# A two-block transformer kernel with 32 experts: a branch that falls through, one more early fetch of rows, four slot tables for sixteen

## The chip, the cores and the metric

The kernel runs on one core of a Trainium2 chip. A core has five engines, each with its own instruction stream: TensorE (PE) for matrix products, VectorE (DVE), ScalarE (ACT), GpSimd (POOL) and SyncE (SP), which here only starts transfers. Sixteen DMA engines carry the transfers of all queues. A transfer can be put on a hardware queue (by SP or ACT) or on the software queue (by POOL). The metric is device time in microseconds (us), the median of several runs; less is better.

## The reference

Two blocks follow each other on 512 tokens of width 1024. The first is a mixer (sparse attention and a gated MLP) with a feed-forward layer; the second has a differential attention, a mixture of experts and a gated embedding. The change touches the mixture of experts and what follows it:

```python
def moe(xn, w_router, b_router, w_gate, b_gate, w_up, b_up, w_down, b_down):
    logits = (xt @ w_router).astype(jnp.float32) + b_router.astype(jnp.float32)
    top_vals, top_idx = lax.top_k(logits, TOP_K)
    gates = jax.nn.softmax(top_vals, axis=-1).astype(xn.dtype)
    ...
    def expert_block(args):
        xb, e = args
        gt = xb @ w_gate[e] + b_gate[e]
        up = xb @ w_up[e] + b_up[e]
        gt = jnp.minimum(gt, SWIGLU_LIMIT)
        up = jnp.clip(up, -SWIGLU_LIMIT, SWIGLU_LIMIT)
        hdn = (up + 1.0) * (gt * jax.nn.sigmoid(SWIGLU_ALPHA * gt))
        return hdn @ w_down[e] + b_down[e]
    ...
h = h + moe(rms_norm_2(h, ffn_norm[i]), ...)
gate = jax.nn.sigmoid(rms_norm_2(h, ple_gate_norm[i]) @ w_ple_gate[i])
e = rms_norm_2(p[i] @ w_ple_proj[i], ple_post_norm[i])
h = h + gate * e
```

Every expert has three 1024x1024 float32 matrices, 12 MB in all, so the experts' weights are 384 MB.

## The kernel before

**The routing.** From about 900 us the kernel chooses the experts. The experts are worked through as 32 places; places 0 to 2 are experts 0 to 2, the later ones are ordered by how many tokens they have. Each place takes the rows of its tokens into a tile `xg` by an indirect DMA of POOL (`gather`, L1499). For the first three places the token numbers are found by a product with a one-hot matrix (`one_hot`, `slot_products`, `tokens_of`). Place 0 reads its rows from `base`, the rows before the norm, and DVE scales them afterwards (`scale_rows`); place 1 reads from `normed`, which holds the scaled rows and whose last quarter is written late (`store_normed(0)`). For the other 29 places POOL scatters one entry for each token and each of its four choices into tables in memory (`scatter_entries`, L1578): 16 indirect DMAs of 128 entries, each into a table of its own. Later ACT loads the 16 tables back (`table_slots`, L1768, 64 KB each), and DVE adds them (`sum_tables`, L1774).

**The stream of weights.** `seq` lists 768 steps (matrix, place, k) of 512 KB of weights. SP loads two steps at a time (1 MB, L1545) into one of ten raw buffers; for each step ACT rounds the weights to a high part `whi` and DVE computes the rest `wlo` (both L297), each into a slot of a ring. PE then makes three products a step (L326 to L328, two matmuls of 512 columns each), or two where the place has at most 64 tokens (L1733, L1734). `fetch(i + 6)` stands ahead of step i, so the splits run about five steps ahead. A raw buffer is loaded again when its second `wlo` is done. The order of PE, DVE, ACT and POOL is the order of the program; `put(i, f)` hangs a piece of other work `f` on step i. SP's loads go in order too, and each load also waits until the hardware semaphore that it will signal is free again. There are eight of these (DMAHW0 to 7 in the lists below), taken in turn by all hardware transfers, SP's and ACT's.

```python
for i, (n, p, k) in enumerate(seq):
    fetch(i + 1 + SPLIT_AHEAD)
    for f in beside[i]:
        f()
    ...
```

`begin[1]` is 16, so before the change the table loads hang on steps 24 to 27, the sums on 32, 33 and 34; `turn_rows(1)`, which turns the rows of place 1 on PE (L1703), hangs on step 10.

**Behind the experts.** A place takes at most 112 rows. Where an expert has more, a general path (a loop with branches over all experts, `tc.If(any_over > 0)`, L2111) computes the rest; with these inputs it is never taken. Behind it stands the last stage: SP loads the experts' results (`yb`, L2128), POOL and DVE add them to the rows (`first_sums`, `pair_up`, `add_rows`), PE multiplies by the gate's weights `w_pg`, which SP loaded before the branch (L2023, 512 KB each, eight of them).

Of the kernel before, what the change touches and what calls it, by code (L numbers as in the profile page):

```python
# [21 lines left out]
P = 128  # L22
S = 512
D = 1024
NT = 4
# [214 lines left out]
def build(tc, I, out, dbg=None, stop=None):  # L240
# [3 lines left out]
    with es:  # L244
# [558 lines left out]
        def attention(g, fill):  # L803
# [7 lines left out]
            for i in range(len(units) + AHEAD):  # L811
# [4 lines left out]
                if i in fill:  # L816
# [20 lines left out]
                  {forward - 1: [f"g{i}" for i in range(3)], mixer - 1: [f"p{i}" for i in range(5)], experts - 1: ['x0', 'x1', 'e0']}, {"g": mixer - 1, "p": mixer + 3}, mixer)  # L837
# [434 lines left out]
        tables = [dram.tile([P * NE, 4], F32, name=f"table{j}") for j in range(4 * NT)]  # L1272
# [201 lines left out]
        nc.gpsimd.memset(lower[0:P - SMALL].bitcast(F32), 0.0)  # L1474
# [8 lines left out]
        slots = {}  # L1483

# [13 lines left out]
        def gather(p, src, m, ap):  # L1498
            nc.gpsimd.indirect_dma_start(out=xg[:m], out_offset=None, in_=src, in_offset=bass.IndirectOffsetOnAxis(ap=ap, axis=0),  # L1499
                                         bounds_check=S - 1, oob_is_err=False)  # L1500
# [75 lines left out]
        def scatter_entries(js):  # L1576
            for j in js:
                nc.gpsimd.indirect_dma_start(out=tables[j], out_offset=bass.IndirectOffsetOnAxis(ap=place[:, j // 4, j % 4:j % 4 + 1], axis=0), in_=entry[:, j // 4, j % 4], in_offset=None,  # L1578
                                             bounds_check=P * NE - 1, oob_is_err=False)
# [45 lines left out]
        slot_products(ptok, oh0, (1, 2, 3), 4, told)  # L1625
        weigh(2)
# [11 lines left out]
        gi0 = tokens_of(ptok, 0)  # L1638

        gather(0, base, CAP, gi0)  # L1640
        norm0 = early.tile([P, 4], F32, name="norm0")[:CAP]
        nc.vector.tensor_copy(norm0, ptok[:CAP, 0:4])
        nc.vector.tensor_tensor(out=norm0[:, 3:4], in0=norm0[:, 1:2], in1=norm0[:, 2:3], op=ALU.add)
# [119 lines left out]
        def table_slots(q):  # L1763

            if q == 0:
                sums.extend(row_tile("tabs").rearrange("p (j f) -> p j f", j=8) for _ in range(2))
            for j in range(4 * q, 4 * q + 4):
                nc.scalar.dma_start(sums[j // 8][:, j % 8], tables[j].rearrange("(s e) c -> s (e c)", e=NE))  # L1768

        sums = []  # L1770

        def sum_tables(h):
            tab = tabs[h] = row_tile("tab")[:, :4 * NE].rearrange("p (e c) -> p e c", c=4) if h else early.tile([P, NE, 4], F32, name="tab")
            nc.vector.reduce_sum(tab.rearrange("p e c -> p (e c)"), sums[h].rearrange("p j f -> p f j"), axis=AX)  # L1774
# [3 lines left out]
        def all_slots():  # L1778
            tab = tabs[0]
            nc.vector.tensor_tensor(out=tab, in0=tab, in1=tabs[1], op=ALU.add)  # L1780
# [12 lines left out]
        def turn_rows(p):  # L1793
            pts["x", p] = turned(xg, cap[p])
# [124 lines left out]
        put(11, split_rows, 1)  # L1919
        put(14, gates_by_expert)  # L1920
# [45 lines left out]
        scatter_entries(range(15, 10, -1))  # L1966
# [3 lines left out]
        gather(1, normed, CAP, gi1)  # L1970
        scatter_entries(range(10, -1, -1))
# [139 lines left out]
        with tc.If(any_over > 0):  # L2111
            with tc.tile_pool(name="op", bufs=1, side="right") as op:
                with tc.For_i(0, NE) as e:
                    n_e = nc.values_load(count[0:1, bass.ds(e, 1)], min_val=0, max_val=S, skip_runtime_bounds_check_because="a count of 512 tokens at most")
                    for r in range(-(-(S - SMALL) // P)):
                        with tc.If(n_e > P * r):
                            overflow_rows(op, e, r)


        with pool("fin", 2, side="right") as wp:  # L2120
# [30 lines left out]

            def add_rows(tt):
                h, yb = hs[tt], ybs[tt]
                for cs in pieces(tt):
                    pair_up(tt, cs)
# [56 lines left out]
            for tt in range(NT):  # L2212
                ps = ps_pair()
                if tt == 0:
# [3 lines left out]
                    for c in range(4):  # L2218
# [10 lines left out]
                    turn_rows_of(1)  # L2229
# [48 lines left out]
```

## Time and profile before

| | us |
|---|---|
| median of 3 runs | 2075.75 (2075.34 to 2076.8) |
| profiled execution, whole | 2073.2 |
| profiled execution, span from first to last instruction | 2071.5 |
| PE busy | 1968.3 (95%) |
| DVE busy | 1640.3 (79%) |
| ACT busy | 1370.9 (66%) |
| mean granted clock of PE | 0.985 of full speed |

The span is one execution under the profiler; 1.7 us of that execution lie around it. Busy shares are means over stages with different limits: the expert stage, from about 930 to 1990 us, is half of the time, and most of the change lies at its two ends.

### The profile page before, as it was taken

How to read it: one execution, taken by the hardware profiler on the slowest of the kernel's cores; microseconds unless marked ns; L12 is line 12 of the kernel's file. 1: busy time of each engine (PE TensorE's matmuls, PEld its weight loads, DVE VectorE, ACT ScalarE, POOL GpSimd, SP SyncE). 2: the span in 40 equal slices, each digit the busy share in tenths (PEclk: the TensorE clock that was granted, in tenths of full speed). 3: DMA queues.
4: the chain of work that ended last, by engine and by line, in shares of the span. 5: the costliest groups of instructions: out<-in, count | busy, mean ns of one | idle time of the engine just before them, and what ended most of it. 6: DMA issues, size and time to landing. Idle time of an engine off the chain costs nothing. (4 is left out here: it accounts for less than half of the span.)

```text
span 2071.5 us, 28687 instructions
## 1 busy us (share of the span) xinstructions
PE 1968.3 (95%) x9675; PEld 1507.0 (73%) x9676; DVE 1640.3 (79%) x2290; ACT 1370.9 (66%) x1889; POOL 414.6 (20%) x363
## 2 busy tenths in 40 slices
PE   8999999999999888878999999999999999999968
PEld 6777779888878887666777777777667766767546
DVE  6688874223466666678999999999999999999965
ACT  5656753222355364537799988888888888888942
POOL 0100120000010334124223444322211003201122
PEclk9999999999999998989999999999999999999989
DMA  5510464233555402248999999999999999999973
GB/s 215 173 31 22 176 230 154 91 102 102 182 202 191 129 11 72 107 173 338 403 410 406 412 406 407 402 404 402 405 396 403 399 398 402 398 407 398 365 270 106
DMA packets 113158, 554.16 MB, mean 268 GB/s; under 512 B 16739, under 2 KB 25955, under 8 KB 63852
## 3 DMA queue, kind: packets, MB, share of 16 engines
q1 hardware_dynamic: 90528, 510.04, 63.6%
q10 hardware_dynamic: 15116, 25.40, 3.6%
q0 software_dynamic: 7360, 16.82, 2.4%
q8 instruction: 78, 1.28, 0.2%
q14 instruction: 76, 0.62, 0.1%
HBM read 532.62 MB, written 26.66 MB: 270 GB/s over the span
## 5 line engine op out<-in xcount | busy, mean ns | idle before, releaser
L297 DVE TENSOR_TENSOR wlo<-wraw,whi 128x1024 fp32r<-128x1024 f32 x923 | 1076.1, 1215 | 209.4 <-ACT whi L297 203.8
L297 ACT CAST whi<-wraw 128x1024 fp32r<-128x1024 f32 x923 | 923.1, 1049 | 217.2 <-PE po L327 28.0
L1715 POOL DMA_INDIRECT ybuf<-yt,si x31 | 190.6, 6150 | 453.4 <-ACT yt L1820 453.4
L326 PE MATMUL pw<-whi,xe 128*112 128x512 f32 x544 | 215.9, 397 | 0.0
L327 PE MATMUL pw<-wlo,xe 128*112 128x512 f32 x544 | 214.4, 394 | 0.1
L328 PE MATMUL pw<-whi,xe 128*112 128x512 f32 x544 | 214.0, 393 | 0.0
L1734 PE MATMUL pw<-wlo,xe 128*64 128x512 f32 x406 | 162.9, 401 | 8.6 <-DVE wlo L297 8.0
L1733 PE MATMUL pw<-whi,xe 128*128 128x512 f32 x406 | 161.3, 397 | 3.2 <-DVE xe L297 3.2
L332 POOL TENSOR_SCALAR rstd<-ss 128x1 f32<-128x1 f32 (+1 forms) x68 | 24.8, 364 | 626.9 <-DVE ss L877 387.5
L326 PE MATMUL pw<-whi,he 128*112 128x512 f32 x320 | 128.1, 400 | 0.0
L1499 POOL DMA_INDIRECT xg<-normed,gi x31 | 62.5, 2017 | 327.2 <-PE tr L1703 284.8
L327 PE MATMUL pw<-wlo,he 128*112 128x512 f32 x320 | 126.4, 395 | 0.2
L328 PE MATMUL pw<-whi,he 128*112 128x512 f32 x320 | 126.2, 394 | 0.0
L328 PEld LDWEIGHTS pw<-whi,xe 128*112 128x112 f32 x544 | 94.7, 174 | 31.6
L326 PEld LDWEIGHTS pw<-whi,xe 128*112 128x112 f32 x544 | 94.7, 174 | 31.2
L327 PEld LDWEIGHTS pw<-wlo,xe 128*112 128x112 f32 x544 | 94.8, 174 | 30.9 <-DVE wlo L297 0.7
L1733 PEld LDWEIGHTS pw<-whi,xe 128*128 128x128 f32 x406 | 76.4, 188 | 34.2 <-DVE xe L297 3.6
L1734 PEld LDWEIGHTS pw<-wlo,xe 128*64 128x64 f32 x406 | 54.5, 134 | 46.4 <-DVE wlo L297 31.1
L1733 PE MATMUL pw<-whi,he 128*128 128x512 f32 x182 | 74.1, 407 | 0.0
L1734 PE MATMUL pw<-wlo,he 128*64 128x512 f32 x182 | 72.9, 401 | 0.0
L326 PE MATMUL pa<-x2T,whi 128*128 128x512 f32 (+1 forms) x200 | 72.6, 364 | 0.1
L327 PE MATMUL pa<-x2T,whi 128*128 128x512 f32 (+1 forms) x200 | 72.6, 363 | 0.0
(617 smaller groups left out, 4212.7 us busy)
## 6 DMA issues: line engine op xcount, KB each, us to landing
wraw<-in_we_gate_dram SPq DMA_DIRECT2D x128, 1024.0 KB, 20.4
wraw<-in_we_up_dram SPq DMA_DIRECT2D x128, 1024.0 KB, 21.5
wraw<-in_we_down_dram SPq DMA_DIRECT2D x128, 1024.0 KB, 20.4
wraw<-in_w_gu_dram SPq DMA_DIRECT2D x44, 512.0 KB, 3.8
wraw<-in_w_down_dram SPq DMA_DIRECT2D x44, 512.0 KB, 4.5
wraw<-in_w_out_dram SPq DMA_DIRECT2D x24, 512.0 KB, 5.6
yb<-ybuf SPq DMA_DIRECT2D x6, 1024.0 KB, 8.7
wraw<-in_w_v_dram SPq DMA_DIRECT2D x10, 512.0 KB, 3.9
```

Source lines behind the costliest of these rows:

```text
L297: return nc.scalar.copy(hi, src), nc.vector.tensor_tensor(out=lo, in0=src, in1=hi.bitcast(F32), op=ALU.subtract)
L326: nc.tensor.matmul(o, a[0], b[0], start=start, stop=False)
L327: nc.tensor.matmul(o, a[0], b[1], start=False, stop=False)
L328: W["mm"] = nc.tensor.matmul(o, a[1], b[0], start=False, stop=stop)
L332: ins = nc.gpsimd.tensor_scalar(out=r[:, :w], in0=ss, scalar1=1.0 / n, scalar2=eps, op0=ALU.mult, op1=ALU.add)
L1499: nc.gpsimd.indirect_dma_start(out=xg[:m], out_offset=None, in_=src, in_offset=bass.IndirectOffsetOnAxis(ap=ap, axis=0), bounds_check=S - ...
L1715: nc.gpsimd.indirect_dma_start(out=ybuf, out_offset=bass.IndirectOffsetOnAxis(ap=ap, axis=0), in_=y_, in_offset=None, bounds_check=4 * S - ...
L1733: nc.tensor.matmul(ps[:, cs], a[:, k, 0:P], hi, start=first, stop=False)
L1734: nc.tensor.matmul(ps[:m, cs], a[:, k, 0:m], lo, start=False, stop=False)
```

## The change

Five edits come together.

1. The two tables of the scatters: 16 tables become 4, scatter j writes into table j % 4 (each token has a place of its own in each, so nothing is overwritten but zeros). All 16 scatters stand in one row, ahead of place 0's products. The four tables are loaded by POOL, hung on step 20, and summed by one reduction at step 26.
2. The rows of place 1 are gathered right behind those of place 0, from `base`, into a tile `x1` of their own, and scaled on DVE. Their one-hot matrix lies in the tile `lower`, whose clearing moves to step 12.
3. The room for `x1` is a slot of the ring of split weights (`e0`), which then has one slot less.
4. `tc.If` is told not to prefer its body as the block that follows directly.
5. In the last stage POOL's first additions of a tile (`pair_rows`) stand a tile ahead, and the turning of tile 1's rows stands behind the loads.

```diff
-                  {forward - 1: ..., experts - 1: ['x0', 'x1', 'e0']}, ...
+                  {forward - 1: ..., experts - 1: ['x0', 'x1']}, ...
...
-        tables = [dram.tile([P * NE, 4], F32, name=f"table{j}") for j in range(4 * NT)]
+        tables = [dram.tile([P * NE, 4], F32, name=f"table{j}") for j in range(4)]
...
-        nc.gpsimd.memset(lower[0:P - SMALL].bitcast(F32), 0.0)
+        x1 = W["e0"].tile([P, D], F32, name="x1")
+        nc.gpsimd.memset(x1, 0.0)
...
+        def fetched(p):
+            return x1 if p == 1 else xg
...
+        oh1, ptok1, told1 = lower[:, :NT * CAP].rearrange("p (t c) -> p t c", c=CAP), ps_tr(1), []
+        one_hot(slot_of[:, :, 1:2], (1, 2, 3), oh1)
+        slot_products(ptok1, oh1, (1, 2, 3), 4, told1)
...
         one_hot(slot_of[:, :, 0:1], (0,), oh0)
+        one_hot(slot_of[:, :, 1:2], (0,), oh1)
         slot_products(ptok, oh0, (0,), 4, told)
+        slot_products(ptok1, oh1, (0,), 4, told1)
...
-        gather(0, base, CAP, gi0)
...
+        gis = [tokens_of(ptok, 0), tokens_of(ptok1, 1)]
+        norms_of = []
+        for p, pt in enumerate((ptok, ptok1)):
+            gather(p, base, CAP, gis[p])
...
         places()
-        oh1, ptok1 = new_one_hot(), ps_tr(1)
-        one_hot(slot_of[:, :, 1:2], range(NT), oh1)
-        slot_products(ptok1, oh1, range(NT), 2, [])
-        gi1 = tokens_of(ptok1, 1)
         fetch(2)
-        for cs in (slice(0, 512), slice(512, D)):
-            scale_rows(xg[:CAP, cs], xg[:CAP, cs], norm0[:, 3:4], gpre[:CAP, cs])
+        for p in range(2):
+            x = fetched(p)[:CAP]
+            for cs in (slice(0, 512), slice(512, D)):
+                scale_rows(x[:, cs], x[:, cs], norms_of[p][:, 3:4], gpre[:CAP, cs])
...
+        def load_tables():
+            rows["tabs"] = row_tile("tabs")[:, :16 * NE].rearrange("p (j f) -> p j f", j=4)
+            for j in range(4):
+                nc.gpsimd.dma_start(rows["tabs"][:, j], tables[j].rearrange("(s e) c -> s (e c)", e=NE))
...
+        put(12, lambda: nc.gpsimd.memset(lower[0:P - SMALL].bitcast(F32), 0.0))
...
-        for q in range(4):
-            put(begin[1] + 8 + q, table_slots, q)
-        for h in range(2):
-            put(begin[1] + 16 + h, sum_tables, h)
+        put(20, load_tables)
+        put(begin[1] + 10, sum_tables)
         put(begin[1] + 18, all_slots)
...
-        scatter_entries(range(15, 10, -1))
+        scatter_entries(range(15, -1, -1))
         keep_warm(10, bias[:, 0:P], bias[:, 0:512])
         turn_rows(0)
         split_rows(0)
-        gather(1, normed, CAP, gi1)
-        scatter_entries(range(10, -1, -1))
...
-        with tc.If(any_over > 0):
+        with tc.If(any_over > 0, preferred_fallthrough_block=False):
...
+                            pair_rows(1)
                             sums[1] = on_chip_rows(1)
                             add_rows(1)
...
+                if tt + 2 < NT:
+                    pair_rows(tt + 2)
+                if tt == 0:
+                    turn_rows_of(1)
```

**POOL around the first gathers.** In the lists below each row is a line of the program, an operation, what it writes and reads, and the semaphores that it waits for (DMASW0 to 7 are those of POOL's own transfers, DMAHW0 to 7 those of SP's and ACT's). Before, from the gather of place 0 on:

```order
L1499 DMA xg<-base,gi_9002 112x1024 [waits DMAHW5_49,DMAHW7_49,DMAHW2_49,DVE_49]
L1578 DMA table_8109<-entry,place 4096x4 [waits DVE_49]
L1578 DMA table_8108<-entry,place 4096x4 [waits DMAHW4_49]
L1578 DMA table_8107<-entry,place 4096x4 [waits DMAHW3_49]
L1578 DMA table_8106<-entry,place 4096x4
L1578 DMA table_8105<-entry,place 4096x4 [waits DMAHW1_49]
L1499 DMA xg<-normed,gi_9035 112x1024 [waits DMAHW1_49,DMAHW0_49,DMAHW3_49,DMASW0_49,DMAHW5_49,DVE_49,PE_49]
L1578 DMA table_8104<-entry,place 4096x4
L1578 DMA table_8103<-entry,place 4096x4
L1578 DMA table_8102<-entry,place 4096x4 [waits DMASW1_49]
L1578 DMA table_8101<-entry,place 4096x4 [waits DMASW2_49]
```

After, from the same gather on (`x_8621` is `x1`):

```order
L1503 DMA xg<-base,gi_8986 112x1024 [waits DMAHW3_49,DMAHW6_49,DMAHW1_49,DVE_49]
L1503 DMA x_8621<-base,gi_8990 112x1024 [waits DVE_49]
L1582 DMA table_8097<-entry,place 4096x4 [waits DVE_49]
L1582 DMA table_8096<-entry,place 4096x4 [waits DMAHW0_49]
L1582 DMA table_8095<-entry,place 4096x4
L1582 DMA table_8094<-entry,place 4096x4
L1582 DMA table_8097<-entry,place 4096x4 [waits DMASW2_49]
L1582 DMA table_8096<-entry,place 4096x4 [waits DMASW3_49]
L1582 DMA table_8095<-entry,place 4096x4 [waits DMASW4_49,DMASW0_49]
L1582 DMA table_8094<-entry,place 4096x4 [waits DMASW5_49,DMASW1_49]
L1582 DMA table_8097<-entry,place 4096x4 [waits DMASW6_49]
L1582 DMA table_8096<-entry,place 4096x4 [waits DMASW7_49]
```

The gather of place 1 moved up from behind five scatters to directly behind the first, and reads `base`. Each scatter from the fifth on now waits for the landing of the scatter four ahead of it, which wrote the same table. The row goes on after the change to the gather of place 2 and the table loads:

```order
L1582 DMA table_8095<-entry,place 4096x4 [waits DMASW4_49]
L1582 DMA table_8094<-entry,place 4096x4 [waits DMASW5_49]
L1925 MEMSET lower 64x1024 [waits PE_49]
L1503 DMA xg<-normed,gi_9221 112x1024 [waits DMAHW4_49,DMAHW5_49,DMAHW1_49,DMAHW7_49,DVE_49,PE_49]
L1776 DMA tabs<-table_8094 128x128 [waits DMASW1_49]
L1776 DMA tabs<-table_8095 128x128 [waits DMASW0_49]
L1776 DMA tabs<-table_8096 128x128 [waits DMASW7_49]
L1776 DMA tabs<-table_8097 128x128 [waits DMASW6_49]
```

The four table loads stand between the gathers of places 2 and 3, each behind the last scatter into its table.

**SP around the branch.** L2111 is `tc.If` before, L2113 after; `most` is the count on which it branches. Before:

```order
L2023 DMA wraw<-in_w_pg_dram 128x1024 [waits DMAHW5_49,PE_49]
L2023 DMA wraw<-in_w_pg_dram 128x1024 [waits DMAHW6_49,DVE_49,PE_49]
L2110 TENSOR_LOAD most [waits DVE_49]
L2111 COMPARE_AND_BRANCH
...
L2111 UNCONDITIONAL_BRANCH [waits SP_sequencer_49,DMAHW0_49,DMAHW1_49,DMAHW2_49,DMAHW3_49,DMAHW4_49,DMAHW5_49,DMAHW6_49,DMAHW7_49]
L2128 DMA yb<-ybuf 128x4x256 [waits DMASW3_49,DMASW4_49,DMASW2_49,DMASW5_49,DMASW1_49,DMASW6_49,DMASW0_49,DMASW7_49,DVE_49,DMAHW7_49,PE_49,Activation_49]
```

The branch jumps over the general path, some 220 rows left out at the dots, to a block that waits for all eight hardware semaphores. After:

```order
L2025 DMA wraw<-in_w_pg_dram 128x1024 [waits DMAHW0_49,PE_49]
L2025 DMA wraw<-in_w_pg_dram 128x1024 [waits DMAHW1_49,DVE_49,PE_49]
L2112 TENSOR_LOAD most [waits DVE_49]
L2113 COMPARE_AND_BRANCH
L2113 UNCONDITIONAL_BRANCH [waits SP_sequencer_49,DMAHW0_49,DMAHW1_49,DMAHW2_49,DMAHW3_49,DMAHW4_49,DMAHW5_49,DMAHW6_49,DMAHW7_49]
...
L2025 DMA wraw<-in_w_pg_dram 128x1024 [waits DMAHW2_49,PE_49]
L2130 DMA yb<-ybuf 128x4x256 [waits DMASW3_49,DMASW4_49,DMASW2_49,DMASW5_49,DMASW1_49,DMASW6_49,DMASW0_49,DMASW7_49,DVE_49,DMAHW3_49,PE_49,Activation_49]
```

The waiting block now follows the branch directly, and ends in an unconditional branch over the general path, the same rows left out at the dots. One load of `w_pg` that stood ahead of the branch now stands behind it, ahead of the first `yb`. PE, DVE, ACT and POOL have the same two branches in the same order, with their own part of the general path between.

## Rows read from the trace of the kernel before

**Rows 1.** page, part 1, of TensorE
```profile
PE 1968.3 (95%) x9675; PEld 1507.0 (73%) x9676; DVE 1640.3 (79%) x2290; ACT 1370.9 (66%) x1889; POOL 414.6 (20%) x363
```

**Rows 2.** windows of the expert stage: engines' busy time, granted clock, DMA share, GB/s
```profile
1000.00:1200.00 200.00, 200.00 (x925) 145.91 (x924) 199.19 (x191) 178.75 (x200) 75.00 (x13) 1.00 1.01 406
...
1400.00:1600.00 200.00, 196.30 (x886) 139.57 (x885) 191.67 (x183) 172.54 (x191) 36.56 (x12) 1.00 1.01 401
```

**Rows 3.** timeline of PE: start, us, what, idle before and its releaser
```profile
927.57 0.99 PE L1703 MATMUL tr<-ident,xg 112*128 112x112 f32 x8
...
938.87 0.52 PE L1495 MATMUL tr<-info,oh 128*112 128x2 f32 x4 [2.69 <-DVE oh L1488]
...
951.35 1.73 PE L1703 MATMUL tr<-ident,xg 112*128 112x112 f32 x8 [4.46 <-DMA xg<-normed,gi]
...
955.04 0.40 PE L326 MATMUL pw<-whi,he 128*112 128x512 f32 x1
955.28 0.40 PE L327 MATMUL pw<-wlo,he 128*112 128x512 f32 x1
```

**Rows 4.** timeline of DVE, same stretch and columns
```profile
925.17 1.40 DVE L352 SCALAR_TENSOR_TENSOR xg<-xg,norm,g_ffn_norm 112x512 f32<-112x512 f32 x2
...
952.94 1.37 DVE L297 TENSOR_TENSOR xe<-tr,xe 128x448 fp32r<-128x448 f32 x2 [3.71 <-ACT xe L297]
```

**Rows 5.** timeline of POOL, same columns
```profile
921.28 1.12 POOL L1578 DMA_INDIRECT table<-entry,place  x1 [4.03 <-DVE place L1574]
...
937.10 5.93 POOL L1499 DMA_INDIRECT xg<-normed,gi  x1 [8.48 <-DVE wlo L297]
943.33 1.09 POOL L1578 DMA_INDIRECT table<-entry,place  x1 [0.30 <-issue]
...
959.27 1.44 POOL L1578 DMA_INDIRECT table<-entry,place  x1 [0.30 <-issue]
```

**Rows 6.** line L1578, the scatters: time from issue to landing
```profile
DMA to landing us min/median/max: 2.1/6.1/8.3
```

**Rows 7.** windows of the dip and of the stretch behind it
```profile
960.00:990.00 30.00, 30.00 (x140) 22.86 (x139) 28.11 (x36) 21.02 (x24) 1.73 (x2) 1.00 0.80 286
1000.00:1050.00 50.00, 50.00 (x233) 36.76 (x232) 49.94 (x49) 41.68 (x47) 12.61 (x3) 1.00 1.01 404
```

**Rows 8.** waits of SP, 955 to 985: us, times, longest
```profile
SPq L1545 <- DMA tabs<-table: 17.2, 3, 10.7
```

**Rows 9.** timeline of DVE, the table sums
```profile
987.15 1.98 DVE L1774 TENSOR_REDUCE tab<-tabs 128x128 f32<-128x1024 f32 x1
```

**Rows 10.** page, part 6: DMA issues, KB each, median us to landing
```profile
wraw<-in_we_gate_dram SPq DMA_DIRECT2D x128, 1024.0 KB, 20.4
...
wraw<-in_w_gu_dram SPq DMA_DIRECT2D x44, 512.0 KB, 3.8
```

**Rows 11.** DMA issues from 1004 to 1046, same columns
```profile
wraw<-in_we_gate_dram SPq DMA_DIRECT2D x8, 1024.0 KB, 9.0
```

**Rows 12.** line L2111, the branch: ns min/median/max, first and last start
```profile
L2111 SPq EVENT_SEMAPHORE  x9: 17/17/17, 1988.7 to 1993.7; - x9
...
L2111 ACTq EVENT_SEMAPHORE  x2: 17/17/17, 1990.3 to 1990.4; - x2
...
L2111 SPq COMPARE_BRANCH  x1: 50/50/50, 1982.3 to 1982.3; - x1
L2111 PEldq COMPARE_BRANCH  x1: 7026/7026/7026, 1987.0 to 1987.0; - x1
...
L2111 ACTq COMPARE_BRANCH  x1: 45/45/45, 1988.8 to 1988.8; - x1
```

**Rows 13.** timeline of SP behind the branch
```profile
1994.60 2.96 SPq L2128 DMA_DIRECT2D yb<-ybuf  x4
```

**Rows 14.** windows around the branch
```profile
1990.00:1995.00 5.00, 0.53 (x1) 0.50 (x2) 1.64 (x2) 2.47 (x3) 0.00 (x0) 0.50 0.27 98
```

**Rows 15.** timeline of POOL in the last stage
```profile
2025.20 6.65 POOL L2150 TENSOR_TENSOR yb<-yb 128x512 f32<-128x512 f32 x4
```

More of the change, by code (lines that the diff above doesn't have):

```diff
@@ L836, in build @@
         open_ring("ring2", stages + ["h"] * (NE * 24), lambda u: 2 if u < experts - 1 else SPLIT_AHEAD if u >= experts else 0,
-                  {forward - 1: [f"g{i}" for i in range(3)], mixer - 1: [f"p{i}" for i in range(5)], experts - 1: ['x0', 'x1', 'e0']}, {"g": mixer - 1, "p": mixer + 3}, mixer)
+                  {forward - 1: [f"g{i}" for i in range(3)], mixer - 1: [f"p{i}" for i in range(5)], experts - 1: ['x0', 'x1']}, {"g": mixer - 1, "p": mixer + 3}, mixer)
         if stop == "mix":
@@ L1498, in gather @@
         def gather(p, src, m, ap):
-            nc.gpsimd.indirect_dma_start(out=xg[:m], out_offset=None, in_=src, in_offset=bass.IndirectOffsetOnAxis(ap=ap, axis=0),
+            nc.gpsimd.indirect_dma_start(out=fetched(p)[:m], out_offset=None, in_=src, in_offset=bass.IndirectOffsetOnAxis(ap=ap, axis=0),
                                          bounds_check=S - 1, oob_is_err=False)
@@ L1577, in scatter_entries @@
             for j in js:
-                nc.gpsimd.indirect_dma_start(out=tables[j], out_offset=bass.IndirectOffsetOnAxis(ap=place[:, j // 4, j % 4:j % 4 + 1], axis=0), in_=entry[:, j // 4, j % 4], in_offset=None,
+                nc.gpsimd.indirect_dma_start(out=tables[j % 4], out_offset=bass.IndirectOffsetOnAxis(ap=place[:, j // 4, j % 4:j % 4 + 1], axis=0), in_=entry[:, j // 4, j % 4], in_offset=None,
                                              bounds_check=P * NE - 1, oob_is_err=False)
@@ L1637, in build @@
             nc.tensor.matmul(pn, ones, chosen[:, t2], start=t2 == 0, stop=t2 == NT - 1)
-        gi0 = tokens_of(ptok, 0)
-        gather(0, base, CAP, gi0)
-        norm0 = early.tile([P, 4], F32, name="norm0")[:CAP]
-        nc.vector.tensor_copy(norm0, ptok[:CAP, 0:4])
-        nc.vector.tensor_tensor(out=norm0[:, 3:4], in0=norm0[:, 1:2], in1=norm0[:, 2:3], op=ALU.add)
+        gis = [tokens_of(ptok, 0), tokens_of(ptok1, 1)]
+        norms_of = []
+        for p, pt in enumerate((ptok, ptok1)):
+            gather(p, base, CAP, gis[p])
+            t = early.tile([P, 4], F32, name=f"norm{p}")[:CAP]
+            nc.vector.tensor_copy(t, pt[:CAP, 0:4])
+            nc.vector.tensor_tensor(out=t[:, 3:4], in0=t[:, 1:2], in1=t[:, 2:3], op=ALU.add)
+            norms_of.append(t)
         weigh(0)
@@ L1761, in fold_lower, with sum_tables @@
                 W["mm"] = nc.tensor.matmul(ps[:SMALL, cs], fold, lower[:, cs], start=False, stop=True, skip_group_check=True)
[L1763 to L1774, printed above, removed]
+        def load_tables():
+            rows["tabs"] = row_tile("tabs")[:, :16 * NE].rearrange("p (j f) -> p j f", j=4)
+            for j in range(4):
+                nc.gpsimd.dma_start(rows["tabs"][:, j], tables[j].rearrange("(s e) c -> s (e c)", e=NE))
+        def sum_tables():
+            tab = tabs[0] = early.tile([P, NE, 4], F32, name="tab")
+            nc.vector.reduce_sum(tab.rearrange("p e c -> p (e c)"), rows.pop("tabs").rearrange("p j f -> p f j"), axis=AX)
         tabs = {}
@@ L1779, in all_slots @@
             tab = tabs[0]
-            nc.vector.tensor_tensor(out=tab, in0=tab, in1=tabs[1], op=ALU.add)
             gi, si = rows_of(early, tab[:, :, 1], tab[:, :, 2], NE)
@@ L1793, in turn_rows @@
         def turn_rows(p):
-            pts["x", p] = turned(xg, cap[p])
+            pts["x", p] = turned(fetched(p), cap[p])
         def split_rows(p):
@@ L2150, in pair_up, with pair_rows @@
                     nc.gpsimd.tensor_tensor(out=ybs[tt][:, z, cs], in0=ybs[tt][:, z, cs], in1=ybs[tt][:, z + 1, cs], op=ALU.add)
+            def pair_rows(tt):
+                for cs in pieces(tt):
+                    pair_up(tt, cs)
             def add_rows(tt):
                 h, yb = hs[tt], ybs[tt]
-                for cs in pieces(tt):
-                    pair_up(tt, cs)
                 nc.vector.tensor_tensor(out=h, in0=h, in1=sums[tt], op=ALU.add)
@@ L2228, in build @@
                     gate_product(0, ps, both, range(6, 8))
-                    turn_rows_of(1)
                 if tt + 2 < NT:
```

## The prediction

> **What bounds the kernel now.** I read the page first. PE is busy for 95% of the span [rows 1], so whatever shortens the time shortens PE's waits or the work that feeds PE. The windows of the expert stage, which is half of the time, come next [rows 2]: from 1000 to 1200 us PE is busy for all of 200 us, DVE for 199.19, and the DMA engines are full at 406 GB/s; from 1400 on PE has holes (196.30 of 200) while the DMA engines stay full at 401 GB/s. So three resources run at their limit together, and the one that ends the stage is the stream of weights. The issues show the same: a load of 1 MB takes 9.0 us to land just after 1000 [rows 11] and 20.4 us in the median of the whole stage [rows 10]. Loads are issued further and further ahead of what the DMA engines can carry. Work saved on PE or DVE in the middle is then worth nothing; what counts is how many bytes the stream has carried before it becomes full, and how soon the last stage starts.
>
> Then I read the timelines of the stretch in which the stream starts, and its windows. From 960 to 990 us the DMA engines move 286 GB/s, from 1000 to 1050 us 404 GB/s [rows 7]. In between lies a hole: SP's next weight load waits for table loads, 17.2 us in three waits [rows 8]. The 16 table loads that ACT issues take hardware semaphores in turn with SP's loads, and SP's queue is in order, so weights stand behind small loads that are late. At the other end I read the line of the branch [rows 12] and what SP issues behind it [rows 13].
>
> **The front, part by part.** *Table loads off ACT's queue.* The hole is worth (404 - 286) x 30 us = 3.54 MB, at 404 GB/s 8.8 us. Twelve tables of 64 KB fewer are 0.79 MB, 1.9 us more. If the whole of it came back, the stream would be 10.7 us earlier. It can't all come back: loads can only be issued when PE, and DVE behind it, free the raw buffers, and PE was not waiting in that hole (30.00 of 30 us busy).
>
> *Rows of place 1 earlier.* PE waits 4.46 us for the gather from `normed`, and then turns the rows at 1.73 us where place 0's took 0.99 [rows 3]; from 951.35 to 955.04 it does that turn and six matmuls, which at the distance of two starts there (0.23 us) and 0.99 for the turn would have taken 2.4 us instead of 3.7. Together 4.46 + 1.3 = 5.8 us. After the change the rows are in `x1` some 20 us before they are wanted, so PE gets all of it: step 11 starts at about 949.3 and not at 955.0. The other wait of PE there, 2.69 us for the third one-hot matrix, is DVE's [rows 3] and stays; it also hides what the start may lose at a lower clock, since PE's warming matmuls now run earlier and PE then idles before place 0, as it idled before the slow turn at 951.35.
>
> *DVE.* It loses two more scalings, 1.40 us as place 0's are, and gains its idle time of 3.71 us at place 1 [rows 4], and one reduction in place of two, of half the size (1.98 us each [rows 9], so about 3 us saved). It is ahead, and so no new bound. Place 0 itself starts as before: its scaling comes about half a microsecond earlier, since the wait for the second one-hot product is gone from DVE's queue behind the scatter addresses, and the scaling of `x1` delays what follows by about as much.
>
> *How much the stream gains.* Just after 1000 us a load takes 9.0 us [rows 11]; a lone load of 1 MB would take about 3.8 us, as a lone one of 512 KB does [rows 10], and 1.3 us for the other half at 404 GB/s, so 5.1. The loads there are issued 3.9 us earlier than needed. With the issues 5.8 us earlier, the stream can be 9.7 us earlier before it starves. The ring of split slots is one shorter, so a split may come one step later (six matmuls, 1.4 us) and with it the free raw buffer; whether the ring is what holds it, no row shows, so the price is between 0 and 1.4. I take all of it: 8.3 us, less than the 10.7 that the hole offers. The bounds are 4.4 (PE's gain less the slot, no reserve) and 10.7.
>
> *Scatters and tables.* The scatters start about 1.3 us later than 921.28 [rows 5], behind DVE's extra small operations. Each scatter from the fifth on waits for the landing of one four ahead. Before, eleven of them ran at (959.27 - 943.33) / 10 = 1.59 us each [rows 5], and landing took 6.1 us, at most 8.3 [rows 6]. A group of four then takes the longer of 6.4 and about 7.2 us; three groups and the last four end at 922.6 + 21.6 + 6.4 = 951, with the longest landing 957; before, the last ended at 960.7. Behind them stand the gather of place 2 and four table loads, each 1 to 1.5 us of POOL, landing at 963 to 968. The sum hangs on step 26, 15 steps of 1.4 us behind 949.3, at about 970. So it is hidden, with 2 to 7 us to spare. If it weren't, DVE would stand still there with the splits behind it.
>
> **The tail, part by part.** *The branch.* Today SP reaches it at 1982.3, gets to its first wait at 1988.7 and to the last at 1993.7, and issues `yb` from 1994.60 [rows 12, 13]. The 6.4 us after the branch lie beside the landing of the last weights. PE's branch takes 7.03 us, ACT's 1.5 (1988.8 to 1990.3) [rows 12]. After the change SP waits first and then jumps over the same general path, so whatever the jump costs on SP is no longer hidden by the landing. From 1990 to 1995 us only 0.49 MB move (98 GB/s) [rows 14], about the eighth load, which now stands behind the branch; so the waits end between 1990.0 and 1992.4 (one load of 1.3 us less), I take 1991.2. Then come the jump F, one load's issue of 0.74 us [rows 13], and `yb`; before, `yb` came 0.9 us behind the waits. The eighth load's bytes ahead of `yb` cost 1.3 us less that 0.74. That makes F + 1991.2 + 0.9 + 1.3 - 1994.6 = F - 1.2. For F no row is without other transfers: 6.4 on SP and 7.03 on PE while the weights were landing, 1.5 on ACT at their end. Behind the waits nothing else moves, so I go by ACT's row and add one for the longer path: F = 2.5, and the tail is 1.3 us later. Bounds: F = 0 and 1990.0 give -2.4, F = 6.4 and 1992.4 give +5.2 to +6.4.
>
> [...]
>
> *Additions a tile ahead.* POOL's four additions take 6.65 us [rows 15] and now run before they are wanted. PE is busy through that stretch but for waits of 0.3 us, so I take 0.2.
>
> **The sum.** The profiled execution took 2073.2 us. -8.3 + 1.3 - 0.2 = -7.2 gives 2066.0. The median of the runs shown is 2.55 us above that execution, so I predict 2068.5 against 2075.75. A change under 0.2% (4.15 us) can't be told from none.
>
> **The rivals.** *The tail takes it back* (place: SP behind the waits). If F is 6.4 as on SP today, the tail is 5.2 later, the sum -3.3: 2072.4, no change that can be told. For it speaks that SP's own row has that number; against it, that it was measured under a full load.
>
> *Only PE's part comes back* (place: raw buffers). If SP still can't issue earlier than PE frees buffers and the reserve is used up by jitter, the front gives 4.4 and the time is 2075.75 - 4.4 + 1.3 - 0.2 = 2072.4. The full 30 us of PE in the hole speak for it.
>
> *Tables too late, slower.* The four table loads now go by POOL's queue, beside DVE at its limit. The gather at 937.10 took 5.93 us of POOL where the scatter behind it took 1.09 [rows 5], and its rows landed at 951.35, 14 us after. If the last table lands so late, at about 961 + 14 = 975 or, with issues of 5.93 us for the four, at 984 or more, DVE stands still from 970 on. A stall of DVE up to 8.3 - 1.1 = 7.2 us only eats the gain; beyond it every microsecond is lost to the stream, and at 984 the time is 2075.75 + 14 - 7.2 = 2082.5. The scatters beside the same splits took 1.09 to 1.44 us, so I give it a small chance. [...]
>
> *No stall at all behind the waits.* If the jump finds its code at hand, F = 0, the tail gains 1.2 to 2.4, and with the whole hole 10.7 the time is 2075.75 - 12.1 to -13.3: 2062.4 to 2063.6.
>
> **Chances.** Forecast 0.5; the tail takes it back 0.15; only PE's part 0.15; tables too late 0.1; no stall 0.1. The forecast with its own bounds runs from 2064 to 2072; the range that leaves out the late tables and the best corner is 2062.5 to 2076. Faster by over 0.2% takes the forecast (0.45 of its 0.5), the best case and a third of the two middle rivals, 0.65; within 0.2% 0.25; slower 0.1, the late tables alone.
>
> **What would show it.** In the changed kernel's profile: SP's weight loads go on from 960 to 990 us without waits for tables, at 380 GB/s or more; PE turns place 1's rows without a wait near 947; the scatters are done by 957 and DVE's one reduction starts without idle time near 970. In the tail SP's waits come right behind the branch, then a stall of 1.5 to 4 us, then one load of `w_pg` and `yb`; PE's stall of 7 us stays, but ends before its first product can start. I am wrong if the rate in that window stays under 350 GB/s, if DVE waits for the tables, or if the last stage, from the last expert's product to the end, is over 4 us longer than before.

## The result, and the profile after

The changed kernel takes 2057.14 us in the median of 4 runs (2054.02 to 2060.58) against 2076.12 us before, run beside it. The ratio is taken as 0.9913, with a 95% interval from 0.9901 to 0.9926: faster by 0.9%, some 18 us. The forecast was 2068.5 us in a range from 2062.5 to 2076, so the sign was right and the gain more than twice as large as forecast. The profiled execution took 2054.02 us (span 2052.2).

The windows of the changed kernel, with the columns of [rows 2] and [rows 7]:

```profile
960.00:990.00 30.00, 30.00 (x140) 22.86 (x139) 29.79 (x42) 23.39 (x26) 1.00 (x1) 1.00 0.96 364
1000.00:1200.00 200.00, 200.00 (x920) 145.37 (x919) 196.67 (x189) 179.61 (x199) 81.90 (x12) 1.00 1.01 405
1400.00:1600.00 200.00, 200.00 (x920) 145.52 (x919) 199.42 (x192) 178.06 (x198) 100.34 (x14) 1.00 1.01 411
```

The hole between 960 and 990 us is nearly closed (364 GB/s against 286; the prediction had named 380 or more). But there is something that no part of the forecast has: from 1400 to 1600 us the stream moves 411 GB/s against 401, and PE has no holes there. The DMA engines were busy all the time in both kernels (share 1.01), so they carry more in the same busy time.

What answers to [rows 3] to [rows 5] and [rows 8], [rows 9], from the timelines of PE, DVE and POOL (start, us, what, idle before and its releaser) and SP's waits from 955 to 985 us:

```profile
936.41 0.52 PE L1499 MATMUL tr<-info,oh 128*112 128x2 f32 x4 [0.76 <-DVE oh L1492]
...
944.31 0.93 PE L1713 MATMUL tr<-ident,x 112*128 112x112 f32 x8
```

```profile
946.75 1.15 DVE L297 TENSOR_TENSOR xe<-tr,xe 128x448 fp32r<-128x448 f32 x2
...
970.47 1.09 DVE L1780 TENSOR_REDUCE tab<-tabs 128x128 f32<-128x512 f32 x1
```

```profile
919.50 1.74 POOL L1582 DMA_INDIRECT table<-entry,place  x1 [2.66 <-DVE place L1578]
...
947.99 1.90 POOL L1582 DMA_INDIRECT table<-entry,place  x1 [0.30 <-DMA wraw<-in_we_up_dram]
...
954.74 2.24 POOL L1776 DMA_DIRECT2D tabs<-table  x4 [2.52 <-DMA table<-entry,place]
```

```profile
SPq L1549 <- DVE wlo L297: 11.7, 5, 3.9
SPq L1549 <- DVE gate_of L1879: 11.1, 3, 4.7
SPq L1549 <- DVE gi L1694: 2.2, 1, 2.2
```

PE turns the rows of place 1 at 944.31 without a wait. The last scatter is issued at 947.99, the four tables at 954.74, and DVE's sum at 970.47 has no idle time before it. SP waits only for DVE, which frees raw buffers, and no longer for tables.

At the other end, the line of the branch (as [rows 12]) and SP's timeline behind it (as [rows 13]):

```profile
L2113 SPq EVENT_SEMAPHORE  x9: 17/17/116, 1958.3 to 1968.1; - x9
...
L2113 SPq COMPARE_BRANCH  x2: 38/46/53, 1958.2 to 1968.2; - x2
L2113 PEldq COMPARE_BRANCH  x2: 95/3129/6163, 1963.1 to 1963.5; - x2
```

```profile
1954.99 16.33 SPq L2025 DMA_DIRECT2D wraw<-in_w_pg_dram  x6
1971.74 2.87 SPq L2130 DMA_DIRECT2D yb<-ybuf  x4
```

SP's waits end at 1968.1 and its second branch, the jump, starts at 1968.2. The sixth load of `w_pg` in the first row is the one behind the branch; the row ends at 1971.32, so that load is issued at about 1971.0: the jump costs SP 2.8 us, PE 6.16.

### The profile page after: what moved, and what is told of

It reads as the page before. It is cut to its first block, busy times and chain, and to the rows that moved or that the text cites. A ratio compares the mean times of both kernels' runs of the same rounds, so it can differ in the third digit from the quotient of the medians.

```text
span 2052.2 us, 28296 instructions
## 1 busy us (share of the span) xinstructions
PE 1966.1 (96%) x9675; PEld 1514.0 (74%) x9676; DVE 1634.3 (80%) x2293; ACT 1375.7 (67%) x1889; POOL 526.1 (26%) x368
## 5 line engine op out<-in xcount | busy, mean ns | idle before, releaser
L1725 POOL DMA_INDIRECT ybuf<-yt,si x31 | 279.8, 9027 | 362.1 <-ACT yt L1825 362.1
L1503 POOL DMA_INDIRECT xg<-normed,gi x30 | 78.0, 2599 | 280.2 <-PE tr L1713 252.1
L328 PE MATMUL pa<-x2T,wlo 128*128 128x512 f32 (+1 forms) x200 | 72.6, 363 | 0.0
```

Of the source, the lines that this page charges most:

```text
L328: W["mm"] = nc.tensor.matmul(o, a[1], b[0], start=False, stop=stop)
L1503: nc.gpsimd.indirect_dma_start(out=fetched(p)[:m], out_offset=None, in_=src, in_offset=bass.IndirectOffsetOnAxis(ap=ap, axis=0), bounds_ch ...
L1725: nc.gpsimd.indirect_dma_start(out=ybuf, out_offset=bass.IndirectOffsetOnAxis(ap=ap, axis=0), in_=y_, in_offset=None, bounds_check=4 * S - ...
```

## The experiments

All ratios are against the kernel before, run on the same chip beside the kernel in question. There its median went from 2072.0 to 2075.3 us, so kernels are compared by their ratios and not by their medians. Two theories stood at the start: that the further gain is the stream's lead (L, later P: PE is earlier, and the state in which the stream becomes full lasts), or that the packets' rate changes from run to run (R). Two more came up on the way: the number of slots in the ring (S), and the address of the raw buffers (A).

| kernel | edit | ratio (95%) | median us |
|---|---|---|---|
| b_copy | before, unchanged | 1.0000 (0.9991 to 1.0008) | 2072.2 |
| b_if | before + branch | 1.0011 (1.0002 to 1.0020) | 2075.8 |
| b_tables | before + four tables | 0.9987 (0.9977 to 0.9996) | 2070.8 |
| b_rows | before + early rows, ring one shorter | 0.9943 (0.9930 to 0.9956) | 2059.7 |
| b_slot16 | before, ring without e0 | 1.0016 (1.0006 to 1.0025) | 2079.2 |
| b_slot16x | before, ring without x1 | 0.9999 (0.9989 to 1.0010) | 2075.0 |
| a_slot17 | changed, e0 back in the ring | 0.9913 (0.9900 to 0.9926) | 2056.6 |
| a_if_off | changed, branch as before | 0.9913 (0.9900 to 0.9926) | 2057.5 |
| b_pad32 | before + 32 unused bytes | 0.9942 (0.9929 to 0.9954) | 2061.1 |
| b_padE | before + 32 bytes under the buffers alone | 0.9948 (0.9934 to 0.9962) | 2061.8 |
| a_pad32 | changed + 32 unused bytes | 0.9974 (0.9962 to 0.9986) | 2068.3 |
| a_pad64 | changed + 64 unused bytes | 0.9975 (0.9966 to 0.9985) | 2068.5 |
| a_pad128 | changed + 128 unused bytes | 0.9957 (0.9941 to 0.9972) | 2066.2 |
| a_align | changed, other three buffers moved by 32 | 0.9906 (0.9892 to 0.9920) | 2055.1 |
| a_align256 | changed, all ten on multiples of 256 | 0.9913 (0.9891 to 0.9935) | 2055.2 |
| b_rows_pad32 | b_rows + 32 unused bytes | 0.9995 (0.9985 to 1.0006) | 2072.9 |
| a_tables_off | changed, sixteen tables as before | 0.9953 (0.9938 to 0.9968) | 2064.4 |
| a_best | a_align256, additions as before | 0.9904 (0.9886 to 0.9922) | 2054.1 |

**The parts by themselves.** The control first.

> The kernel before, unchanged, as a control. In the changed kernel's trace the 8 KB packets of the weight stream take 309 ns in the median behind 1000 us, in the trace of before 313 ns, and the stream moves 409 us-rate GB/s against 401 from 1400 to 1800 us. Theory R (rate by chance): the packet time differs from run to run of one and the same program; then this copy shows 309 ns in its trace or its times spread by several us. Theory L (lead): it belongs to the program; then the copy shows 313 ns, 401 GB/s from 1400 to 1800 us and 2075 to 2077 us again.

The copy is the same as before, and its weight packets take 313 ns again. Theory R falls: the packet time belongs to the program.

> Before with the branch edit alone. My prediction: SP's jump is no longer hidden by the landing of the last weights, +1.3 us (from -2.4 to +6.4). The comparison of the two traces says more: from PE's last expert matmul to the end the changed kernel takes 89.1 us against 84.4, so this edit alone should cost about 4.7 us if the tail's loss is the branch's; 0 if it is a later effect of the other edits.

```diff
-        with tc.If(any_over > 0):
+        with tc.If(any_over > 0, preferred_fallthrough_block=False):
```

Alone it costs 0.1%, some 2 us, in the range that the prediction gave (1.3, from -2.4 to 6.4); the 4.7 us of the last stage are not all the branch's.

> Before with the four tables, loaded by POOL and summed once, alone (the gather of place 1 stays between the scatters). Theory L: the stream's hole from 960 to 990 us goes, weight loads are issued as PE frees buffers; PE's wait at place 1 stays, so the issues are no earlier than before and the stream gains only its reserve, 2 to 4 us. Rival: the stream alone sets the end, and the whole hole of 8.8 us and the 1.9 us of the twelve tables come back, 10 us or more.

```diff
-        tables = [... for j in range(4 * NT)]
+        tables = [... for j in range(4)]
...
+        put(20, load_tables)
+        put(begin[1] + 10, sum_tables)
```

Its hole is gone, in the window from 960 to 990 us (columns as above), but PE still waits 4.51 us for place 1 (PE's timeline):

```profile
960.00:990.00 30.00, 30.00 (x141) 22.84 (x140) 29.61 (x42) 21.62 (x25) 6.28 (x8) 1.00 0.97 366
```

```profile
950.24 1.51 PE L1703 MATMUL tr<-ident,xg 112*128 112x112 f32 x8 [4.51 <-DMA xg<-normed,gi]
```

The kernel gains 2.7 us (0.8 to 4.8 by the interval), as much as theory L had, but hardly in the stream: from the issue of place 0's gather, load 84 starts 225.7 us later (225.3 in before, 225.6 in the copy) and the last one 1036.6 (in the kernels that leave the front as it was, 1036.9 to 1038.4). Without earlier issues the stream can't use the time that the hole took. The first load itself starts at 816.2 us, in the copy at 818.9; over the ten kernels with four tables the mean is 817.5, over the eight with sixteen, b_slot16 and b_slot16x apart, 819.1. Twelve tables fewer are zeroed ahead of it, but no run tries that alone. Both theories put a gain into the stream that hardly shows there, and where the 2.7 us lie stays open.

> Before with the early gather of place 1, its own tile and the ring one slot shorter, alone (sixteen tables, loaded by ACT). Theory L: PE gains 5.8 us at place 1, but the hole of the table loads stays and the stream is full behind it, so the end moves by less than 2 us. Rival: PE sets the end, and its 5.8 us come back in full.

```diff
+        x1 = W["e0"].tile([P, D], F32, name="x1")
...
+        for p, pt in enumerate((ptok, ptok1)):
+            gather(p, base, CAP, gis[p])
+            t = early.tile([P, 4], F32, name=f"norm{p}")[:CAP]
```

This gave 11.8 us, twice what PE's wait is worth, and neither theory had that. Its packets take 309 ns, like the changed kernel's, so something in this edit sets the stream's rate.

**The ring.** The edit also makes the ring of slots one shorter.

> Before with the ring of split slots one shorter (16 slots for 17, e0 left unused), nothing else. The early rows alone gave 0.994 and their trace has weight packets of 309 ns where all kernels with 17 slots have 313 from about 1000 us on. Theory S (slots): the ring's length makes the difference of the packets, so this kernel shows 309 ns and 405 to 411 GB/s from 1400 to 1800 us, and is 7 to 10 us faster than before. Theory P (PE earlier): the rate comes from the stream's state at its start; then this kernel shows 313 ns and is within 2 us of before, or slower by up to 1.4 us, as my prediction had it.

> Before with 16 slots again, but x1 left out of the ring and e0 kept in it. Theory S by number: the same gain as with e0 left out. Theory S by place (e0 lies beside the raw buffers): 313 ns and no gain.

> The changed kernel with e0 given to the ring as a 17th slot from step 12 on, when the rows of place 1 are turned. Theory S by number: packets of 313 ns again, 401 GB/s from 1400 to 1800 us, 7 to 10 us slower than the changed kernel (2064 to 2068 against 2057). Theory P: same as the changed kernel.

```diff
-                  {..., experts - 1: ['x0', 'x1', 'e0']}, ...
+                  {..., experts - 1: ['x0', 'x1']}, ...
```

Both kernels with 16 slots have 313 ns and gain nothing; in both the stream even starts late (load 0 at 826.9 and 830.0 us). And the changed kernel with 17 slots keeps 309 ns and its time. Theory S falls. With 16 slots the eighth load of `w_pg` finds no slot ahead of the branch. In SP's timeline of b_slot16 the six loads behind the first two end at 1993.1, and `yb` follows at 1994.62, level with [rows 13]:

```profile
1978.08 15.05 SPq L2023 DMA_DIRECT2D wraw<-in_w_pg_dram  x6
1994.62 2.63 SPq L2128 DMA_DIRECT2D yb<-ybuf  x4
```

b_slot16 is 0.16% slower than before and b_slot16x not; with the branch as before, what that load costs is too small for a price from the two. That it stands behind the branch comes from the ring (edit 3) and not from the branch (edit 4): in a_if_off, which has the branch as before, it stands there too, in a_slot17 it doesn't.

> The changed kernel with the branch as it was. The branch edit alone cost 2.3 us on before (1.0011). If it costs the same here, 2055 us against 2057; by the two traces' tails (89.1 against 84.4 us) up to 4.7 us faster. If the waits and the jump overlap with the end of the stream otherwise here: no difference.

In the changed kernel the branch makes no difference that can be told: the two intervals are nearly the same.

**The address.** What else does b_rows do to the stream? It needs one more small tile, `norm1`, 16 bytes a partition, which takes 32 in a pool below the raw buffers. In the listing of the addresses that the program gives its tiles, seven of the ten raw buffers move by 32 bytes:

```text
raw buffers E0 to E6, first address   before 132832 = 518 * 256 + 224
                                      changed 132864 = 519 * 256
raw buffers y0 to y2, first address   190432 = 743 * 256 + 224 in both
```

> Before with one unused tile of 32 bytes a partition in the pool that lies below the raw buffers, nothing else. It moves seven of the ten raw buffers from addresses that are 32 past a multiple of 64 to multiples of 64, as the one small tile norm1 does in the changed kernel. Theory A (address): the weight packets take 309 ns in place of 313, the stream moves 408 to 411 GB/s from 1400 to 1800 us, and the kernel is 8 to 12 us faster than before. Theory P (PE earlier, the stream's state at its start): 313 ns and no difference.

```diff
+        early.tile([P, 8], F32, name="pad")
         fold = early.tile([P, SMALL], F32R, name="fold")
```

An unused tile on the kernel before gives 0.9942, as much as b_rows. Its windows from 1000 to 1200 and 1400 to 1600 us:

```profile
1000.00:1200.00 200.00, 200.00 (x920) 145.61 (x919) 198.81 (x193) 179.10 (x199) 73.59 (x13) 1.00 1.01 409
1400.00:1600.00 200.00, 200.00 (x917) 145.94 (x916) 197.24 (x190) 176.96 (x198) 64.28 (x13) 1.00 1.01 409
```

> Before with 32 unused bytes directly below the seven raw buffers, so that these alone move to multiples of 256; the small tiles, the one-hot tiles and the slot e0 stay where they are. If the raw buffers' address is the cause: 309 ns and 10 to 13 us faster than before, as with the pad below the small tiles. If one of the other tiles that moved with them is: 313 ns and no difference.

```diff
+            if t == "E0":
+                padp = alloc("padp")
+                padp.tile([P, 8], F32, name="pad")
             W[t] = alloc(t)
```

Here the small tiles, the one-hot tiles and e0 stay in place and only the raw buffers move; the gain is the same. It is the address of the buffers into which the weights are written. The engines that read the buffers are no quicker for it: from 1400 to 1600 us a `whi` of ACT takes 1047 ns in before and 1051 in b_padE, a `wlo` of DVE 1215 and 1214. The stream is, in the window of b_padE from 1400 to 1600 us:

```profile
1400.00:1600.00 200.00, 199.77 (x915) 145.66 (x914) 197.08 (x190) 176.53 (x197) 63.67 (x13) 1.00 1.01 409
```

> The changed kernel with the same unused 32 bytes, which put its seven raw buffers back to 32 past a multiple of 64. Theory A: 313 ns, 401 GB/s, 8 to 12 us slower than the changed kernel, 2065 to 2069 us, which is what my prediction summed up without it. Theory P: 2057 us.

The same 32 bytes take most of the gain from the changed kernel, which then stands at 2068.28 us, with the stream at 404 GB/s:

```profile
1400.00:1600.00 200.00, 198.37 (x901) 142.19 (x900) 195.19 (x187) 173.54 (x192) 68.36 (x14) 1.00 1.01 404
```

 This is the five edits without buffers on multiples of 256, the kernel that the prediction summed up.

> The changed kernel with 64 unused bytes: the seven buffers stay on multiples of 64, but not of 128. If 64 is what counts, 309 ns and 2057 us as the changed kernel; if 128 is, 313 ns and 2065 to 2069 us.

> The changed kernel with 128 unused bytes: the seven buffers lie on multiples of 128 and not of 256 (64 past a multiple of 128 gave 312 ns and 2068.5 us). If 128 is what counts: 309 ns and 2057 us. If 256 is: 312 to 313 ns and 2068 us.

With 64 bytes the gain of the address is gone as with 32, with 128 most of it is. From the trace's records of the weight queue, 8 KB packets from 1450 to 1550 us:

| kernel | E0 to E6 past a multiple of 256 | median ns (loads 60 to 379) | share at 308 to 311 ns |
|---|---|---|---|
| before | 224 | 313 | 26% |
| b_rows_pad32 | 32 | 313 | 26% |
| a_pad32 | 32 | 313 | 25% |
| a_pad64 | 64 | 312 | 29% |
| a_pad128 | 128 | 309 to 313 by buffer | 46% |
| b_pad32 | 0 | 309 | 83% |
| b_padE | 0 | 309 | 82% |
| changed | 0 | 309 | 85% |
| a_align256 (y0 to y2 at 0 too) | 0 | 309 | 92% |

So 256 is the multiple that the runs single out, with 128 in between by its packets; by their times a_pad128 and a_pad64 can't be told apart.

> The changed kernel with 32 unused bytes above the other three raw buffers, which puts all ten on multiples of 64. Theory A: their packets fall from 313 to 309 ns too and the kernel is faster by three sevenths of what the seven give, 3 to 5 us, if the stream still sets the end; less if PE does. Theory P: no difference.

> The changed kernel with the other three raw buffers moved too (224 unused bytes above them), so that all ten lie on multiples of 256. If the three still cost something: their packets at 309 ns, mean of all under 319.5 ns (320.3 in the changed kernel), and 1 to 4 us faster than the changed kernel. If the seven were enough: same as the changed kernel, 2055 to 2057 us.

Moving the other three buffers raises the share of short packets, and the medians are 2 us lower, but the intervals cover the changed kernel's.

**The edits apart from the address.**

> The early rows of place 1 and the ring one shorter, alone on before, with 32 unused bytes that put the raw buffers off again (32 past a multiple of 128). By the address theory the edit's 11.8 us were all the address's, since padding alone on before gave 12: 313 ns and within 2 us of before. If PE's 5.8 us at place 1 are worth something by themselves: 3 to 6 us faster than before.

With the buffers off again, the early rows are worth nothing by themselves. PE no longer waits at place 1 (PE's timeline), but the hole stays, with ACT's tables on SP's path (SP's waits, 955 to 990 us, then the window):

```profile
945.55 0.93 PE L1714 MATMUL tr<-ident,x 112*128 112x112 f32 x8
```

```profile
SPq L1550 <- DMA tabs<-table: 17.4, 3, 7.9
```

```profile
960.00:990.00 30.00, 29.80 (x138) 22.29 (x136) 24.54 (x31) 20.29 (x24) 0.00 (x0) 1.00 0.87 328
```

> The changed kernel with the sixteen tables, ACT's loads and the two reductions as before (addresses as in the changed kernel). If the tables give their 2 to 6 us only with the early rows: 2059 to 2063 us against 2057. If they are worth nothing where the stream is fast: 2057 us.

In the changed kernel the tables are worth 0.40%, 8 us: 0.9953 without them, 0.9913 with. That is more than the 2 to 6 us expected.

> The changed kernel with all ten raw buffers on multiples of 256 and without the additions a tile ahead (POOL's additions and the turn of tile 1 as before). The changed kernel's trace has DVE's four additions of tile 1 at 6.91 us beside POOL's of tile 2, and PE waiting 2.2 us for them, where the kernels without this edit have 4.03 us and 0.3 us. If that is the edit's price: 2 to 4 us faster than the same kernel with it, 2051 to 2053 us by the times against 2055.2. If other work takes the wait over: no difference.

The additions a tile ahead make DVE slower at tile 1. In the changed kernel's timelines of POOL, DVE and PE in the last stage:

```profile
1992.56 11.77 POOL L2152 TENSOR_TENSOR yb<-yb 128x512 f32<-128x512 f32 x8
```

```profile
1996.28 6.91 DVE L2163 TENSOR_TENSOR hk<-hk,yb 128x512 f32<-128x512 f32 x4
```

```profile
2003.34 0.63 PE L360 MATMUL tr<-ident,hk 128*128 128x128 f32 x4 [2.18 <-DVE hk L2163]
```

POOL adds the rows of tiles 1 and 2 in one go (eight additions), and beside it DVE's four additions of tile 1 take 6.91 us. In a_best, with the additions as before, DVE takes 4.04 us for them:

```profile
1992.79 4.04 DVE L2162 TENSOR_TENSOR hk<-hk,yb 128x512 f32<-128x512 f32 x4
```

and PE's wait there falls from 2.2 to 0.3 us, as before the change. But POOL's additions of tile 2 then stand beside DVE's next products, and slow them instead: three of four take 1.67 to 1.78 us in a_best, where all four take 0.69 in the changed kernel. One of them in a_best, then in the changed kernel:

```profile
2001.16 1.67 DVE L2195 TENSOR_TENSOR sgm<-sgm,hk 128x512 f32<-128x512 f32 x1
```

```profile
2006.97 0.69 DVE L2196 TENSOR_TENSOR sgm<-sgm,hk 128x512 f32<-128x512 f32 x1
```

So the edit moves some 3 us of DVE's time from one place to another. The time, 0.9904 (0.9886 to 0.9922) against 0.9913 (0.9891 to 0.9935), can't tell the two kernels apart; a_best has the lowest ratio of all, and is not shown to beat the changed kernel.

## Why the prediction was wrong, point by point

**The step that failed** is the first, and unspoken one in the sum: that the full stream goes at the same rate after the change. The prediction called the stream the bound of the stage and priced its lead in bytes at 404 GB/s; it never asked what the change does to the packets. The change moves seven raw buffers by 32 bytes, the packets go from 313 to 309 ns, and over the stretch where the stream sets the pace that is worth 0.5 to 0.6% (b_pad32, b_padE), some 11 us. Neither the diff nor the rows of the kernel before show it; the addresses do. So most of the gain doesn't lie at the two ends of the expert stage, where the edits are, but between them. Why multiples of 256 are what counts, no run shows: the packets take 313 ns at 224 past one and at 32 past one alike.

**The front: right, with the size nearly right.** The issue of place 0's gather, and SP's weight loads number 84 and 383, starts in us from the traces:

| kernel | gather | 84 | 383 | gather to 84 | gather to 383 |
|---|---|---|---|---|---|
| before | 915.9 | 1141.3 | 1953.7 | 225.3 | 1037.8 |
| b_copy | 914.3 | 1139.9 | 1952.7 | 225.6 | 1038.4 |
| b_slot16 | 915.0 | 1142.8 | 1952.1 | 227.9 | 1037.1 |
| b_rows_pad32 | 914.7 | 1140.2 | 1950.0 | 225.6 | 1035.3 |
| b_tables | 914.5 | 1140.3 | 1951.1 | 225.7 | 1036.6 |
| a_pad32 | 914.5 | 1134.1 | 1942.1 | 219.6 | 1027.6 |
| b_pad32 | 915.3 | 1139.7 | 1940.9 | 224.4 | 1025.6 |
| changed | 913.4 | 1133.0 | 1928.9 | 219.5 | 1015.5 |

The first load is no mark to count from: in b_slot16 and b_slot16x it starts late, and from it to the last they take 8 us less than before and gain nothing. Counted from the gather, the edits without the address (a_pad32) have the last load 10.2 us earlier than before and 10.8 earlier than the copy; 8.3 were forecast. By load 84 it is 5.7 to 6.0 us, PE's 5.8, and the rest comes where the stream is full. PE itself reaches step 11 some 33.0 us behind the gather in the changed kernel and 39.1 in before, 6.1 us earlier. Its start at place 0 was slow, as the prediction feared (granted clock 0.50 from 926 to 931 us), and the wait for the third one-hot matrix, 0.76 us for 2.69, took that up. Each half alone gives little or nothing in the stream (b_rows_pad32 2.5 to 3.1 us at the last load, b_tables 1.2 to 1.8, neither any by load 84). That is the rule by which the prediction took the smaller of two bounds: loads can be issued earlier only when PE is earlier, and that helps only when no table loads stand in the queue. The address acts behind load 84: b_pad32 is 1.2 us ahead of the copy there and 12.8 at load 383.

**Scatters and tables: right.** Forecast were an end of the scatters at 951 and the sum hidden at about 970; it was 949.9 and 970.47, without idle time. The rival of late tables did not come.

**The ring one shorter: not needed.** The 1.4 us that I took off the stream's reserve for it aren't seen: the stream gained 10.2 to 10.8 us, 8.3 were forecast with the 1.4 taken off, 9.7 without. On before alone the shorter ring has load 84 2.2 to 2.6 us later, and the last load not.

**The branch: right.** F was taken as 2.5 us and is 2.8; what SP does in that time, no run shows. `yb` is issued 9.3 us behind PE's last expert product (1962.45 to 1971.74), before 8.2 us (1986.38 to 1994.60 [rows 13]): 1.1 us later, 1.3 forecast. Over the ten traces with this edit it is 9.3 us in the mean (8.0 to 10.5), over the ten without it 8.0 (7.1 to 8.6). In the time the edit costs some 2 us on before, and nothing that can be told in the changed kernel.

**The additions: no gain shown.** I took 0.2 us off for them, against [rows 15] alone. They cost PE a wait of 1.9 us more, since POOL's additions beside them slow DVE's (6.91 us for 4.04), and they spare DVE as much a little later. What slows DVE beside POOL, no run shows.

**The last stage: longer than forecast.** From PE's last expert product to the end of the span it takes 89.8 us against 85.1: 4.7 us more, where the sum had 1.1, and over the 4 us that the prediction itself named as a sign of being wrong. The windows of that stretch, before and after, with the columns of [rows 2]:

```profile
1986.38:2071.50 85.12, 66.13 (x288) 49.21 (x288) 49.45 (x66) 22.55 (x35) 24.48 (x24) 0.92 0.53 190
```

```profile
1962.45:2052.20 89.75, 69.71 (x288) 50.86 (x288) 48.58 (x66) 23.68 (x36) 23.33 (x24) 0.86 0.51 183
```

The mean granted clock of PE is 0.86 against 0.92, and the same 288 matmuls keep it busy for 3.6 us longer. One pair of traces can't price the stage, then: the copy of before has 87.0 us at 0.89. Over the ten traces of before and of what was tried on it, the stage takes 85.0 to 88.2 us at a clock of 0.86 to 0.92; over the nine with the additions ahead 87.3 to 95.4 us at 0.81 to 0.91; in a_best 89.9 us at 0.89. That it is longer after the change is shown; how much of that the branch, the additions and the clock each take is not.

**The sum again.** The five edits without the address have 0.9974 (0.9962 to 0.9986), 3 to 8 us, 5.4 in the middle. The sum of 7.2 lies in that, with a front that gave 2 us more than forecast and a last stage that took back more. That a_pad32's 2068.28 us meets the 2068.5 of the prediction so closely is luck: before took 2074.36 us beside it. The other 12 us are the address.

## What to carry to other kernels

Where a stream of transfers sets the time, look at the addresses into which it writes, and put its buffers on multiples of 256 bytes (309 ns a packet for 313 here, and 0.5 to 0.6% of the time, in b_pad32 and b_padE); a small tile that is added or dropped below them moves them, and any edit then comes with a gain or a loss that isn't its own. Before an edit is credited, run the kernel before with its addresses (a pad), and the edit with those of before. And two edits that free the same queue from two sides may be worth little alone and more together: here 1.0 us (not told from nothing) and 2.7 us alone, while taking the tables out of the changed kernel costs 8 us.

## What the runs showed of the hardware that I had not expected

Thirty-two bytes of address change the rate of a stream whose packets are 8 KB: 309 or 313 ns a packet in the median, 409 or 401 GB/s from 1400 to 1600 us on before, 411 or 404 in the changed kernel. The three raw buffers that were not moved (224 past a multiple of 256) have 309 ns too in the changed kernel, and 313 in the kernel before; so the time of a packet isn't set by its own address alone, and why the loads share it is open. Their own address counts a little: 74% of their packets are short in the changed kernel (308 to 311 ns, loads 60 to 379) and 86% of those of the other seven, and with all ten on multiples of 256 it is 91 and 88%. In the kernel before the packets of the first 28 loads have 309 ns at the same addresses, in its copy those of about the first 40, and only the later ones 313; that is open too.
